# S5 operations merged into wider ones, softmax normalisation on another engine, and six projection rows spread over eight attention heads

## The chip, the cores and the metric

The kernel runs on one NeuronCore of a Trainium2 chip. The metric is the device time of one execution in microseconds; the time of the kernel before is the median of three runs. A NeuronCore has five engines that work side by side: TensorE (PE, matrix products from SBUF into PSUM; PEld is its weight load), VectorE (DVE), ScalarE (ACT), GpSimd (POOL) and SyncE (SP, which issues the weight transfers). Each engine executes its own instructions in order and waits for others through semaphores.

## The reference, cut to what matters

Two layers of a streaming encoder on 272 tokens (16 meta tokens and 256 frames) of width 2048. The change touches only the mixer of the first layer. It projects the tokens once, gives 1024 columns to a diagonal state-space model (S5) and the rest to eight heads of latent attention, and projects both results back:

```python
proj = h @ w_in
a_out = s5_mixer(proj[..., :o1], ...)
b_out = mla_mixer(proj[..., o1:o2], proj[..., o2:o3], proj[..., o3:], ...)
return jnp.concatenate([a_out, b_out], axis=-1) @ w_out
```

S5, per group of 16 channels with 64 complex states, is a linear recurrence over the tokens; `f` is a complex factor of each state that scales `b`:

```python
bb_re = f_re[..., None] * b_re - f_im[..., None] * b_im
bb_im = f_re[..., None] * b_im + f_im[..., None] * b_re
...
_, _, s_re, s_im = lax.associative_scan(_complex_affine_combine, (a_seq_re, a_seq_im, bu_re, bu_im), axis=0)
y = einsum(s_re, c_re) - einsum(s_im, c_im)
y = y.reshape(bsz, n, S5_WIDTH) + d * u
g = jax.nn.gelu(y)
return g * jax.nn.sigmoid(g @ w_glu)
```

Each attention head is a softmax over the visible keys, times the values. Feed-forward networks and a second layer (Mamba-2) follow; nothing in them changes.

## The kernel before, in words

**Matrix products.** Every projection is computed by `linear` (L138). Weights are streamed through `weights` (L112) in chunks of 128 x 1024 (eight tiles of 128 x 128): a DMA into a staging tile `st` (four buffers), a cast by ACT into the high part `hi` (L129), the remainder `lo` by DVE (L130); `hi` and `lo` have three buffers each. Each tile then takes three matmuls of 272 columns (L176, L177, L178). The order of instructions on each engine is set by a scheduler that simulates a timeline over the whole program, so the code order is only its input.

**The stage around the change** is `layer0_mixer` (L591). It computes part of the input projection (`in0b`), the S5 constants (`S5.setup`), the rest of the latents (`in0a`), the q up-projection `uq`, S5 run 0, the k up-projection, the values, S5 run 1, and then a loop over eight heads. For each head h, `scores` (L783) of head h+1 is written first: six matmuls into two banks (`sc_a`, `sc_b`), masks, row maxima (L805, DVE), scaling of the maxima (L806), the exponential (L807, ACT), the reciprocal of the sum (L808) and the normalisation (L809, DVE). `values` (L813) then transposes the probabilities of head h (`pt_a`, L824), copies them (L829) and multiplies by the values (`att_o`, L832). The scores, `pt_a` and the rope share three PSUM banks. After the heads 0 to 5, one row of the input projection (`in0_2` to `in0_7`, 16 tiles, 48 matmuls each) is computed; its result is copied to u by ACT (L669) and starts an S5 run. Heads 6 and 7 have no row.

**One S5 run** (`S5.run`, L1302; q is its number) sends the row of u to memory and back in shifted form (`u2`), multiplies it by `gt` into two PSUM tiles (`w_p`, L1320), turns them by the tables `ec` and `es` (L1326 to L1331, DVE), scans over time (L1337, L1338), turns them back (L1339 to L1345), and computes the output `s5y_p` from u with `kb` (L1350, the local part) and from the states with `ca` (L1354); u is then overwritten (L1357). `w_p`, `s5y_p`, `gt_p` and `kb_p` share two PSUM banks. After that, `prep_pe` (L1267) of run q+1 makes `gt` (transposes L1277, copies L1279), `kb` (L1284, L1289) and the tables, and `prep` (L1234) of run q+2 makes on POOL the constants `gb` and `ca` (products L1256 to L1261, copied by ACT at L1264 and L1265). `cmul` (L1067) is a complex product of six operations; POOL uses it in `prep` and DVE in `prep_pe`, with the same three scratch buffers, of which one is also used by `zsqr` (L1103) in the setup.

**After the heads**, `split` (L209) casts the eight head outputs into `mix`, the second half of the output projection (`out0b`) runs with its evacuation on DVE, ACT applies the GELU to the eight rows of u (after the last head's output), and `glu` and `out0a` follow.

## Time and profile before

| | before |
|---|---|
| median of 3 runs | 2657.0 us (2655.68 to 2657.4) |
| profiled execution | 2660.51 us |
| its span, from first to last instruction | 2658.5 us |
| mean granted TensorE clock | 0.995 |
| instructions | 48273 |

In a row of the profile, a name such as `w_p L1320` is the tile that an instruction writes and its line in the kernel; `x8` is a count. "A <- B" in a list of waits says that instruction A stood still until B was done. A window row gives the busy time of each engine in a stretch of the span, with the granted TensorE clock (1.00 is full speed) and the transfer rate. The stage of the change lies between about 64 and 255 us of the span.

### The profile page before, as it was taken

Reading aid. Unit: us, or ns where it says so; the run is one execution under the profiler, and the core shown is the slowest. Engines: PE = TensorE matmul, PEld = TensorE weight load, DVE = VectorE, ACT = ScalarE, POOL = GpSimd, SP = SyncE. Lnnn points to the kernel's source line nnn. Section 1 sums busy time; section 2 is a strip of 40 time slices with the busy share of each in tenths; the row PEclk is TensorE's granted clock in tenths of the full one; section 3 lists DMA queues with packets and bytes.
Section 4 is the critical chain, followed back from the end, with each engine's and each line's share of the span. In section 5 each row is a group of like instructions: output and inputs, shape, how many; then the busy total and the mean of one; then the engine's idle time right before and its main releaser. Section 6 shows DMA issues by size and latency. Waiting matters only on the chain.

```text
span 2658.5 us, 48273 instructions
## 1 busy us (share of the span) xinstructions
PE 2632.5 (99%) x19358; PEld 2464.3 (93%) x19358; DVE 1744.2 (66%) x3035; ACT 1323.7 (50%) x2188; POOL 261.8 (10%) x350
## 2 busy tenths in 40 slices
PE   9999999999999999999999999999999999999999
PEld 9787999999999999999999999999998888888887
DVE  8877597444444445669777875788975555555565
ACT  5555456333333334447655654554664443444453
POOL 2663040000000000210001000001300000000021
PEclk9998999999999999999999999999999999999999
DMA  6333545555555555545655555544565555555553
GB/s 231 123 118 121 168 157 181 177 176 175 175 175 175 175 175 175 175 162 183 208 180 177 180 177 186 179 160 144 182 196 186 188 190 183 189 190 185 188 184 134
DMA packets 140264, 463.97 MB, mean 175 GB/s; under 512 B 14908, under 2 KB 30844, under 8 KB 139912
## 3 DMA queue, kind: packets, MB, share of 16 engines
q1 hardware_dynamic: 139608, 460.40, 52.5%
q8 instruction: 151, 2.47, 0.4%
q14 instruction: 73, 0.60, 0.1%
q10 hardware_dynamic: 432, 0.49, 0.1%
HBM read 457.56 MB, written 3.28 MB: 173 GB/s over the span
## 4 chain that ended last, share of the span: by engine, by line
PE 88%; DVE 7%; POOL 2%; issue 2%; ACT 1%; DMA 0%; SPq 0%; DVEq 0%; ACTq 0%; POOLq 0%
PE mm_gu_b L173 6%; PE mm_gu_a L173 5%; PE mm_in L173 4%; PE mm_gu_a L178 4%; PE mm_gu_a L177 4%; PE mm_gu_a L176 4%; PE mm_gu_b L178 3%; PE mm_gu_b L176 3%; PE mm_gu_b L177 3%; PE mm_gu_b L174 3%; PE mm_dn_b L173 3%; PE mm_dn_a L173 3%; PE mm_in L177 3%; PE mm_in L178 3%; PE mm_in L176 3%; PE mm_gu_a L174 2%
## 5 line engine op out<-in xcount | busy, mean ns | idle before, releaser
L130 DVE TENSOR_TENSOR lo_gu_b<-st_gu_b,hi_gu_b 128x1024 fp32r<-128x1024 f32 x176 | 215.6, 1225 | 228.8 <-ACT hi_gu_b L129 228.7
L130 DVE TENSOR_TENSOR lo_gu_a<-st_gu_a,hi_gu_a 128x1024 fp32r<-128x1024 f32 x176 | 215.2, 1223 | 178.2 <-ACT hi_gu_a L129 177.9
L129 ACT CAST hi_gu_b<-st_gu_b 128x1024 fp32r<-128x1024 f32 x176 | 184.8, 1050 | 290.4 <-issue 155.7
L129 ACT CAST hi_gu_a<-st_gu_a 128x1024 fp32r<-128x1024 f32 x176 | 184.5, 1049 | 234.3 <-issue 116.4
L173 PE MATMUL mm_gu_b<-m,hi_gu_b 128*128 128x512 f32 x704 | 246.8, 395 | 0.0
L130 DVE TENSOR_TENSOR lo_in<-st_in,hi_in 128x512 fp32r<-128x512 f32 (+1 forms) x268 | 182.1, 708 | 77.1 <-ACT hi_in L129 76.2
L129 ACT CAST hi_in<-st_in 128x512 fp32r<-128x512 f32 (+1 forms) x268 | 158.5, 637 | 128.2 <-PE mm_in L177 42.2
L352 POOL TENSOR_TENSOR ln_s<-ln_s,ln_q 128x272 f32<-128x272 f32 (+1 forms) x58 | 71.4, 1231 | 1442.5 <-ACT ln_q L347 1442.0
L178 PE MATMUL mm_gu_a<-mix,lo_gu_a 128*128 128x272 f32 (+1 forms) x704 | 204.3, 291 | 0.3 <-DVE lo_gu_a L130 0.3
L177 PE MATMUL mm_gu_a<-mix,hi_gu_a 128*128 128x272 f32 (+1 forms) x704 | 203.8, 290 | 0.0
L176 PE MATMUL mm_gu_a<-mix,hi_gu_a 128*128 128x272 f32 (+1 forms) x704 | 203.2, 289 | 0.0
L178 PE MATMUL mm_gu_b<-mix,lo_gu_b 128*128 128x272 f32 x704 | 203.2, 289 | 0.0
L177 PE MATMUL mm_gu_b<-mix,hi_gu_b 128*128 128x272 f32 x704 | 202.7, 288 | 0.0
L176 PE MATMUL mm_gu_b<-mix,hi_gu_b 128*128 128x272 f32 x704 | 202.5, 288 | 0.0
L174 PE MATMUL mm_gu_b<-m,lo_gu_b 128*128 128x256 f32 x704 | 197.2, 280 | 0.0
L173 PE MATMUL mm_gu_a<-m,hi_gu_a 128*128 128x512 f32 x544 | 190.7, 395 | 0.0
L173 PE MATMUL mm_in<-f,hi_in 128*128 128x512 f32 x512 | 181.7, 396 | 0.0
L130 DVE TENSOR_TENSOR lo_dn_a<-st_dn_a,hi_dn_a 128x1024 fp32r<-128x1024 f32 x88 | 107.8, 1225 | 110.4 <-ACT hi_dn_a L129 110.0
L129 ACT CAST hi_dn_a<-st_dn_a 128x1024 fp32r<-128x1024 f32 x88 | 92.3, 1049 | 162.1 <-PE mm_dn_a L177 78.5
L173 PEld LDWEIGHTS mm_gu_b<-m,hi_gu_b 128*128 128x128 f32 x704 | 132.5, 188 | 31.2
L130 DVE TENSOR_TENSOR lo_dn_b<-st_dn_b,hi_dn_b 128x1024 fp32r<-128x1024 f32 x88 | 108.6, 1234 | 74.4 <-ACT hi_dn_b L129 74.0
L129 ACT CAST hi_dn_b<-st_dn_b 128x1024 fp32r<-128x1024 f32 x88 | 92.4, 1050 | 130.4 <-PE mm_dn_b L177 48.6
(555 smaller groups left out, 8586.9 us busy)
## 6 DMA issues: line engine op xcount, KB each, us to landing
st_gu_a<-in_w_gu_a SPq DMA_DIRECT2D x176, 512.0 KB, 3.7
st_gu_b<-in_w_gu_b SPq DMA_DIRECT2D x176, 512.0 KB, 4.0
st_in<-in_w_in SPq DMA_DIRECT2D x140, 512.0 KB, 3.3
st_dn_a<-in_w_dn_a SPq DMA_DIRECT2D x88, 512.0 KB, 3.3
st_dn_b<-in_w_dn_b SPq DMA_DIRECT2D x88, 512.0 KB, 3.3
st_in1h<-in_w_in1h SPq DMA_DIRECT2D x34, 512.0 KB, 3.3
st_out1a<-in_w_out1a SPq DMA_DIRECT2D x32, 512.0 KB, 3.3
st_out0b<-in_w_out0b SPq DMA_DIRECT2D x16, 512.0 KB, 3.8
```

Of the source, the lines that this page charges most:

```text
L129: nc.scalar.copy(hi[:, j:j + w], st[:, j:j + w])
L130: nc.vector.tensor_tensor(lo[:, j:j + w], st[:, j:j + w], hi[:, j:j + w], op=ALU.subtract)
L173: nc.tensor.matmul(ps[m].rearrange("p (a b) -> p a b", a=2), lhsT=wh, rhs=x2, start=st, stop=False)
L174: nc.tensor.matmul(o, lhsT=wl, rhs=xh, start=False, stop=left[m] == 0)
L176: nc.tensor.matmul(o, lhsT=wh, rhs=xh, start=st, stop=False)
L177: nc.tensor.matmul(o, lhsT=wh, rhs=xl, start=False, stop=False)
L178: nc.tensor.matmul(o, lhsT=wl, rhs=xh, start=False, stop=left[m] == 0)
L352: nc.gpsimd.tensor_tensor(st["s2"], st["s2"], q, op=ALU.add)
```

## The change

There are four parts.

- **The loop over the heads.** Rows still follow heads, but the two heads without a row are now 1 and 4 instead of 6 and 7: head 0 has row 2, head 1 none, head 2 row 3, head 3 row 4, head 4 none, and heads 5, 6 and 7 have rows 5, 6 and 7.
- **The normalisation** of the probabilities moves from DVE (`tensor_scalar`) to ACT (`mul`), 24 operations.
- **S5 preparation.** The factor `f` is multiplied into the powers once, in the setup (`fw`, for all 32 states at once), and no longer into `c` in each `prep`. With it go `cmul` and the negated copy `nci`; ACT negates when it copies instead. The fourth power of `gb` (which is one) is copied from `bc` and not multiplied. `zs` gets a buffer of its own, `m4x` becomes one tile for all runs.
- **S5 run.** The two tables become one tile `tab` with three planes (cos, sin, minus cos). A turn is then two products of 544 columns and a sum of 544 (`turned`) instead of four products of 272 and two sums; a run has two turns. The table itself is four products and two sums into `tab`, and a negation by ACT.

The core of the diff:

```diff
@@ layer0_mixer
-                if h < 6:
-                    self.linear(f"in0_{h + 2}", rhs, evac_u, N)
+                if h not in (1, 4):
+                    self.linear(f"in0_{2 + h - (h > 1) - (h > 4)}", rhs, evac_u, N)
@@ scores
-            nc.vector.tensor_scalar(p, p, z, None, op0=ALU.mult)
+            nc.scalar.mul(p, p, z)
@@ S5.zsqr
-        t = self.t("zs", [64], tag="cm2", bufs=1).rearrange("p (r a) -> p r a", r=2)
+        t = self.t("zs", [64], bufs=1).rearrange("p (r a) -> p r a", r=2)
@@ S5.setup
+        fw = self.t("fw", [2, 5, 32])
+        t1, t2 = (self.t(f"fw{c}", [2, 5, 32], tag=f"cm{c}") for c in range(2))
+        for t, c in ((t1, fr), (t2, fi)):
+            v.tensor_tensor(t, pw, c.unsqueeze(1).unsqueeze(1).to_broadcast([P, 2, 5, 32]), op=ALU.mult)
+        v.tensor_tensor(fw[:, 0], t1[:, 0], t2[:, 1], op=ALU.subtract)
+        v.tensor_tensor(fw[:, 1], t1[:, 1], t2[:, 0], op=ALU.add)
@@ S5.prep
-        self.cmul(g, cr, ci, bc[:, :, 2, :], bc[:, :, 3, :], fr, fi, [4, 16])
-        nc.scalar.mul(nci, ci, -1.0)
-        for (o, n, k0, xr, xi, sign) in ((gb, 4, 1, ...), (ca, 5, 0, cr, ci, -1)):
+        for (o, z, k0, n, c) in ((gb, self.pw, 1, 3, 0), (ca, self.fw, 0, 5, 2)):
...
+                if c:
+                    nc.scalar.mul(o[hs, 1, :, 0:n, h, :], t3[hs], -1.0)
+                else:
+                    nc.scalar.copy(o[hs, 1, :, 0:n, h, :], t3[hs])
+                    nc.scalar.copy(o[hs, :, :, 3, h, :], bc[hs, :, 0:2, :].rearrange("p s r j -> p r s j"))
@@ S5.prep_pe
-        self.cmul(g, ec..., es..., gr, gi, er, ei, [4, 9, 8])
+        for r, t in ((0, t1), (1, t2)):
+            e = self.ez[:, r, s].unsqueeze(2).to_broadcast([P, 4, 9, 8])
+            for c in range(2):
+                g.tensor_tensor(t[:, c], gz[:, c].unsqueeze(3).to_broadcast([P, 4, 9, 8]), e, op=ALU.mult)
...
+        nc.scalar.mul(tab[:, 2], tab[:, 0], -1.0)
@@ S5.run
-        v.tensor_tensor(a1, w[0], c, op=ALU.mult)
-        v.tensor_tensor(a2, w[1], s, op=ALU.mult)
-        v.tensor_tensor(b1, w[1], c, op=ALU.mult)
-        v.tensor_tensor(b2, w[0], s, op=ALU.mult)
-        v.tensor_tensor(a1, a1, a2, op=ALU.add)
-        v.tensor_tensor(b1, b1, b2, op=ALU.subtract)
...
+        def turned(o, re, im):
+            v.tensor_tensor(a1, re.unsqueeze(1).to_broadcast(sh), tab[:, 0:2, :, 0:68], op=ALU.mult)
+            v.tensor_tensor(a2, im.unsqueeze(1).to_broadcast(sh), tab[:, 1:3, :, 0:68], op=ALU.mult)
+            v.tensor_tensor(o, a1, a2, op=ALU.add)
+        turned(a1, w[0], w[1])
+        for r in range(2):
+            v.tensor_tensor_scan(z[:, r]..., m4..., a1[:, r]..., 0.0, ALU.mult, ALU.add)
+        turned(z, z[:, 0], z[:, 1])
```

What the scheduler makes of it shows at three places. Before, on PE, behind row 4 (the first line is its last matmul) came the end of the values of head 2 and, between pieces of the next S5 run (`kb_p` and the first half of `w_p`), the scores of head 4 (all but the last scores line is shown); row 5 began eight lines further on:

```order
L178 MATMUL mm_in_4_4_2422<-h_82,lo_in_4_1_2450 128x272
L832 MATMUL att_o<-pt,v 128x272
L832 MATMUL att_o<-pt,v 128x192
L832 MATMUL att_o<-pt,v 128x64
L793 MATMUL sc_a<-qk 80x80
L1284 MATMUL kb_p<-ca_548,gb 32x128 x8
L1320 MATMUL w_p<-u_2210,gt 128x68 x4
L794 MATMUL sc_a<-kr,qrope 80x80
L793 MATMUL sc_a<-qk 128x208
L794 MATMUL sc_a<-kr,qrope 128x208
L793 MATMUL sc_b<-qk 64x272
```

Now, on PE, a piece between row 4 and row 5, where head 4 has no row (`sc_a` are now the scores of head 6, `s5y_p<-ro,ca` are the state products of run 3, `u_2429` is row 4 and belongs to run 4):

```order
L1265 MATMUL gt_p<-ident,gb 128x128 x4
L1339 MATMUL s5y_p<-ro_2197,ca_554 32x67 x32
L1272 MATMUL kb_p<-ca_550,gb 32x128 x8
L1313 MATMUL w_p<-u_2429,gt 128x68 x8
L794 MATMUL sc_a<-qk 80x80
L795 MATMUL sc_a<-kr,qrope 80x80
L794 MATMUL sc_a<-qk 128x208
L795 MATMUL sc_a<-kr,qrope 128x208
L1335 MATMUL s5y_p<-u,kb_551 128x272
L1335 MATMUL s5y_p<-u,kb_551 128x68x3
L1335 MATMUL s5y_p<-u,kb_551 128x68x2
L1335 MATMUL s5y_p<-u,kb_551 128x68
```

Two S5 runs and the scores and values of two heads now stand between these rows; row 5 begins 13 lines after the last one shown.

On DVE, before, run 3 (the tiles `ro`, `vr`, `vi`) with the softmax of a head beside it:

```order
L1327 TENSOR_TENSOR ro_2226<-w_p,es 128x272
L1328 TENSOR_TENSOR ro_2227<-w_p,ec 128x272
L1330 TENSOR_TENSOR ro_2225<-ro_2225,ro_2226 128x272
L808 RECIPROCAL sm<-sm 128x1
L1331 TENSOR_TENSOR ro_2227<-ro_2227,ro_2228 128x272
L808 RECIPROCAL sm<-sm 64x1
L1337 SCALAR_TENSOR_TENSOR vr<-m4x_550,ro_2225 128x272
L809 TENSOR_SCALAR prob<-prob,sm 128x208
L1338 SCALAR_TENSOR_TENSOR vi<-m4x_550,ro_2227 128x272
L809 TENSOR_SCALAR prob<-prob,sm 64x272
L1339 TENSOR_TENSOR ro_2225<-vr,ec 128x272
L1340 TENSOR_TENSOR ro_2226<-vi,es 128x272
```

The same run on DVE now, in the stretch without a row (`lo_in_6_0` is the remainder of the first chunk for row 6, `L1327` are the two scans):

```order
L1321 TENSOR_TENSOR ro_2195<-w_p,tab 128x544
L1322 TENSOR_TENSOR ro_2196<-w_p,tab 128x544
L130 TENSOR_TENSOR lo_in_6_0_2918<-st_in_6_0_2915,hi_in_6_0_2917 128x1024
L1323 TENSOR_TENSOR ro_2195<-ro_2195,ro_2196 128x544
L800 MEMSET sc_a 16x64
L1327 SCALAR_TENSOR_TENSOR ro_2197<-m4x,ro_2195 128x272 x2
L806 TENSOR_REDUCE mx<-sc_a 80x1
L806 TENSOR_REDUCE mx<-sc_b 64x1
L1321 TENSOR_TENSOR ro_2195<-ro_2197,tab 128x544
L1322 TENSOR_TENSOR ro_2196<-ro_2197,tab 128x544
L1292 COPY m4x<-m_437 128x4x67
```

The normalisations (L809 before) are gone from DVE there; the wider products L1321 and L1322 each stand for two.

At the end of the heads, on ACT, before: the last output of a head (`qk`), the table load and the GELU, and the casts of the first chunks of `out0b`:

```order
L1289 COPY kb_549<-kb_p 32x4x32 x4
L834 COPY qk<-att_o 128x272
L754 ACT_TABLE_LOAD
L754 ACTIVATE u<-u 128x272 x7
L210 CAST mix<-qk 128x272
L210 CAST gh<-u 128x272 x4
L210 CAST gl<-u 128x272 x3
L129 CAST hi_out0b_3511<-st_out0b_3509 128x1024
L129 CAST hi_out0b_3543<-st_out0b_3541 128x1024
L129 CAST hi_out0b_3575<-st_out0b_3573 128x1024
```

And now, where row 7 is still to be evacuated (L669) and runs 6 and 7 to be fed (`tab`, `ca`, `gt`, `gb`) when the GELU of the first rows begins:

```order
L755 ACT_TABLE_LOAD
L755 ACTIVATE u<-u 128x272 x5
L129 CAST hi_out0b_3283<-st_out0b_3281 128x1024
L210 CAST gh<-u 128x272 x4
L210 CAST gl<-u 128x272
L1291 ACTIVATE tab<-tab 128x288
L1248 COPY ca_554<-pp_2849 64x20x16 x2
L1267 COPY gt<-gt_p 128x512
L1252 COPY gb<-pp_2835 64x4x3x16 x2
L755 ACTIVATE u<-u 128x272
L129 CAST hi_out0b_3315<-st_out0b_3313 128x1024
L669 COPY u<-mm_in_7_7_3104 128x272
```

The casts of the head outputs (`mix<-qk`, L210) were spread before and now follow as a group of eight right behind the last line shown.

## The prediction

> **What bounds the kernel now.** First the page's busy times and the throttle row of its 40 slices.

> ```profile
> PE 2632.5 (99%) x19358; PEld 2464.3 (93%) x19358; DVE 1744.2 (66%) x3035; ACT 1323.7 (50%) x2188; POOL 261.8 (10%) x350
> PEclk9998999999999999999999999999999999999999
> ```

> TensorE (PE) is busy 99% of the span. Neither kernel changes its matmuls, only their order, so the change can win or lose only PE's idle time and PE time at a reduced clock. One slice shows a reduced clock, the fourth (199 to 266 us): the end of the stage that the diff touches. So next come PE's waits from 60 to 340 us, which spans S5, attention and the start of the output projection (waited-for instruction, us in total, times, longest):

> ```profile
> PE mm_uq L176 <- ACT qk L690: 2.4, 1, 2.4
> PE w_p L1320 <- ACT kb L1289: 2.0, 2, 1.6
> PE w_p L1320 <- DVE mx L806: 2.0, 1, 2.0
> PE rope_sw L632 <- ACT rope_x L630: 1.5, 1, 1.5
> PE s5y_p L1354 <- DVE vr L1344: 0.9, 1, 0.9
> PE s5y_p L1350 <- DVE sm L808: 0.9, 1, 0.9
> PE mm_out0b L178 <- DVE lo_out0b L130: 0.2, 1, 0.2
> ```

> These are all of them: 9.9 us. 3.9 us are early (q up-projection and rope); 5.8 us lie at the bare heads 6 and 7. Then the clock, by windows of 10 us and one of 1 us (window, its length, busy us of PE, PEld, DVE, ACT and POOL, granted clock, DMA share, GB/s):

> ```profile
> 75.00:85.00 10.00, 7.60 (x66) 6.82 (x65) 9.75 (x14) 5.90 (x12) 10.00 (x13) 1.00 0.21 62
> 215.00:225.00 10.00, 5.53 (x103) 3.98 (x102) 9.20 (x26) 3.03 (x11) 5.93 (x8) 0.91 0.20 62
> 225.00:235.00 10.00, 9.02 (x33) 7.09 (x33) 9.78 (x28) 5.95 (x19) 4.40 (x6) 0.50 0.23 58
> 235.00:245.00 10.00, 10.00 (x124) 8.82 (x125) 1.83 (x5) 5.86 (x16) 0.00 (x0) 0.74 0.01 2
> ...
> 223.00:224.00 1.00, 0.00 (x0) 0.00 (x0) 0.78 (x5) 0.00 (x0) 0.92 (x3) 0.59 0.00 0
> ```

> The clock falls to half at about 223.2 us (0.59 is a fifth of the window at 1.00, the rest at 0.50) and stays there through 225 to 235 us, where DVE, busy 9.78 of 10, feeds PE too slowly; half of the next window is still at half clock, though PE has no gap there. Work at half clock takes twice as long: 9.02 / 2 = 4.5 us lost there, 10 x (1 - 0.74) = 2.6 behind it, 0.3 before 225, together 7.4. With the waits that makes **17.3 us of loss** in this stage. It is the most that the change can win; everything after 254 us is gapless PE.

> **The change part by part.** *Spreading the heads.* The bare tail (heads 6 and 7 with S5 runs 5 and 6 and no matmuls to fill) loses 5.8 + 7.4 = 13.2 us. One row is 48 matmuls. Two inner pairs now lose theirs: (1,2) and (4,5), the latter holding S5 runs 3 and 4. What bounds a pair is the chain on DVE and ACT per head against PE's work. The rows:

> ```profile
> L130 DVE TENSOR_TENSOR lo_in<-st_in,hi_in 128x1024 fp32r<-128x1024 f32 x12 | 15.0, 1248 | 8.4 <-ACT hi_in L129 8.3
> L129 ACT CAST hi_in<-st_in 128x1024 fp32r<-128x1024 f32 x12 | 12.6, 1047 | 4.7 <-PE mm_in L177 3.1 <-ACT hi_in L129 0.8 <-DMA st_in<-in_w_in 0.6
> L805 DVE TENSOR_REDUCE mx<-sc_a 128x1 f32<-128x208 f32 x8 | 2.9, 360 | 0.0
> L807 ACT ACTIVATE prob<-sc_a,mx 128x208 f32<-128x208 f32 x8 | 3.5, 433 | 3.7 <-DVE mx L806 3.6
> L1337 DVE TENSOR_TENSOR_SCAN vr<-m4x,ro 128x272 f32<-128x272 f32 x8 | 7.0, 880 | 0.0
> L1082 DVE TENSOR_TENSOR cm<-gz,ez 128x288 f32<-128x288 f32 x8 | 7.6, 945 | 0.0
> ```

> Pair (1,2), counted from the end of row 2's matmuls: the two casts of the next weight chunk come first, because a slot of three is freed there (1.05 ACT, then 1.22 DVE), then reductions and exponentials of head 2 (0.4 + 0.4, three times, in part side by side). The scores of head 3 need the bank that head 2's 128x208 exponential reads; it comes free at about 5.2 us, and PE, with head 2's transposes and the S5 work at hand, gets there at 3.55: **1.7 us idle** (0.5 if the casts hide, 4 if both score banks are late).

> Pair (4,5): the S5 chain is rebuilt from 272-wide into 544-wide operations. No row has that width. Two consecutive quiet 272-wide products start 0.36 us apart:

> ```profile
> 216.08 0.43 DVE L1341 TENSOR_TENSOR ro<-vr,es 128x272 f32<-128x272 f32 x1
> 216.44 0.43 DVE L1342 TENSOR_TENSOR ro<-vi,ec 128x272 f32<-128x272 f32 x1
> ...
> L1330 DVE TENSOR_TENSOR ro<-ro,ro 128x272 f32<-128x272 f32 x8 | 5.1, 636 | 0.0
> L1326 DVE TENSOR_TENSOR ro<-w_p,ec 128x272 f32<-128x272 f32 x8 | 3.5, 432 | 5.8 <-PE w_p L1320 5.8
> ```

> So 544 costs between 0.36 (nothing for the width) and 2 x 0.64 = 1.27 (the slower row twice); I take 0.63, 0.36 and three quarters of it again, near the quiet rows. Both sides of run 3, counted from the end of row 4's matmuls, need PE's own stretches (windows cut at the timeline's starts: the scores of a head, the local S5 product s5y_p, a head's first five transposes; then the gt transposes):

> ```profile
> 212.59:215.41 2.82, 2.82 (x14) 1.00 0.47 176
> 206.59:207.80 1.21, 1.21 (x10) 1.00 0.03 5
> 199.17:199.89 0.72, 0.72 (x8) 1.00 0.00 0
> ...
> 215.41 0.66 PE L1277 MATMUL gt_p<-ident,gb 128*128 128x128 f32 x4
> 217.48 0.33 PE L1354 MATMUL s5y_p<-vr,ca 128*32 128x67 f32 x8 [0.93 <-DVE vr L1344]
> 221.26 1.24 PE L1320 MATMUL w_p<-u,gt 128*128 128x68 f32 x8 [1.55 <-ACT kb L1289]
> 224.45 1.98 PE L1320 MATMUL w_p<-u,gt 128*128 128x68 f32 x8 [1.96 <-DVE mx L806]
> ```

> DVE, in the order of the new program: casts 1.05 + 1.22 + 0.13 between, sum 0.63, two scans of 0.71 (0.36 twice; the group's 0.88 holds stretched ones), two reductions 0.67, two products 1.26, table copy and small operations 0.48, sum 0.63 = 7.5 us. PE has 2.82 + 0.72 + 1.21 and two gt groups of 0.5 (0.66 less its overlapped end) = 5.75 until the state products (the 217.48 row's kind): **1.75 idle**. Then DVE does a reciprocal, four table products and two sums at about 0.46, a reduction and the u update, 3.6 us, until 11.1; only that frees the PSUM bank for the next w_p. PE's state products and kb_p, 1.85 (from 217.48 to 221.26 less the wait of 1.55 and the transposes between, 0.38), end at 9.35: **1.75 idle**. Together 3.5, from 1 (544 at its low end) to 6.4 (the six table operations at 945 instead of 460 ns, 2.9 more). In both waits PE stands in order: behind them are kb_p, w_p(4), head 6's scores and row 5, and behind w_p(4) run 4's whole DVE chain.

> *Normalisations and shared buffers.* The rows of what goes (first three the normalisations, then waits for scratch that DVE and POOL share):

> ```profile
> L809 DVE TENSOR_SCALAR prob<-prob,sm 128x208 f32<-128x208 f32 x8 | 4.5, 557 | 0.1
> L809 DVE TENSOR_SCALAR prob<-prob,sm 64x272 f32<-64x272 f32 x8 | 3.7, 460 | 0.1
> L809 DVE TENSOR_SCALAR prob<-prob,sm 80x80 f32<-80x80 f32 x8 | 2.9, 367 | 0.0
> DVE cm L1081 <- POOL cr L1083: 6.1, 6, 3.5
> POOL cm L1082 <- DVE wz L1108: 16.0, 1, 16.0
> ```

> 24 normalisations, 4.5 + 3.7 + 2.9 = 11.1 us, go from DVE to ACT: per head 1.4 off the one and on the other. ACT, busy 5.95 of 10 us in the window where DVE is 9.78, has the room; if ACT is what PE waits for, it costs up to 1.4 per pair, within the bounds above. DVE's 6.1 us and POOL's 16.0 us of waits end, as do POOL's six 64-wide operations per prep; its gb products shrink from 256 to 192 elements, and ACT gets four small copies or negations instead of one, off PE's path like the rest of a prep that has a whole head to finish. One m4x and one set of tables instead of two or more cost nothing: DVE, which writes them, is also the one that reads them, in order. The weight loads and the u transfers move with their rows, onto queues that are used 0.20 to 0.23 in these windows. The setup gains two DVE products of 320 and two sums of 160 elements, by the rows above 0.25 to 0.45 each, 1.4 us together, hidden by the matmuls of in0a (no wait of PE names its weights); uncovered it would cost its 1.4. Of the early 3.9 us, where ACT's copies were late in a window with DVE and POOL full (9.75 and 10.00), I leave **1.5** (0, if the shorter queues remove it, to 6, if the products add to it).

> *The tail.* Row 7 now stands behind head 7, so run 6's update of u, the GELU and the mix casts of the eight heads come while row 7's and out0b's matmuls run.

> ```profile
> L754 ACT ACT_TABLE_LOAD x1 | 1.3, 1283 | 0.0
> ```

> ACT's queue after the last head is: table load 1.3, five GELUs, a weight cast 1.05, five casts, tables, gt copies, then the eight mix casts that out0b's first matmul needs. kb_p(6) waits 1.0 for u (like the 0.93 of the 217.48 row), w_p(6) 0.9 for the gt copy (between 0.4 and 1.6, the two waits for ACT's kb copies in the list), out0b 1.1 for the casts, the state products of run 6, now among out0b's matmuls, 1.0 to 1.3: **4.0**, from 1 to 6. Run 7 and the gated unit behind it have the last 217 matmuls of out0b as cover, 17 us at the rate of the 235 to 245 window; without it the 5 to 6 us of a run would show.

> *Sum.* 1.5 + 1.7 + 3.5 + 4.0 + 0.5 (small gaps of the kind of the 0.2 row) = 11.2 us, against 17.3: **-6.1 us**. The profiled execution took 2660.51 us (2.0 around its span of 2658.5) and would take 2654.4; it lies 3.5 above the median of the runs, 2657.0, which goes to **2650.9**.

> **Rivals.** *R1, the clock falls in the pair (4,5).* At 223.2 it fell after 3.5 us of idle within 4.75 us (the last two w_p rows: 1.55 and 1.96 with one w_p half between); in the window 75 to 85 PE stood 2.4 us in one piece and kept 1.00. My pair loses 3.5 us within 5.35, 1.85 us of work between: near the edge, on the safe side. If it falls, what follows w_p(4) runs at half: the same operations as from 224.45 to 235 before (0.55 and 9.02 us at half, 4.8 at full clock) and a head's scores, 2.8: +7.6; and the way back costs 2.6 as in the 235 to 245 window: +10.2, 2661.1, and with the table operations slow (2.9) 2664.0. This is the slower side; it decides when the two waits of the pair, with little between, sum to more than 3.5 us within 4.75. [...] Chance of R1 0.30, half of it within 0.2%, half slower.

> *R2, more is gained.* 544-wide near 0.4 and ACT never late: pair and tail halve, 1.5 + 0.8 + 1.8 + 2.0 = 6.1: -11.2, about 2645.8. For it: DVE loses 11.1 us of normalisations and 6.1 of waits. Against: the chain is serial. 0.14.

> *R3, the change does not do what it says.* The stalls only move into the pairs; DVE stays the bound at 9 of 10 us, and the sum stays near 17: 2657 +- 3. 0.14. [...]

> **How the numbers follow.** Forecast 0.42 (its own range 2646 to 2655), R1 0.30, R2 0.14, R3 0.14. 0.2% is 5.3 us, about what a measurement of this kernel tells from no change: below 2651.7 is faster. Of the forecast 0.27 is faster, 0.15 same; R2 is faster; R3 same; R1 0.15 same and 0.15 slower: 0.41, 0.44, 0.15. The range goes from R2's far half (2643) to R1's upper end (2664).

> **What would show it.** Right: no window below clock 1.00 between 60 and 350 us; PE waits of 1 to 2 us at s5y_p(3) and w_p(4); out0b starting 6 us earlier. Wrong: a 0.50 window in the pair (4,5) (R1); the L1321 products above 0.9 us, or the table products still at 0.9 (R3); PE waits beyond 15 us in total. A wait of PE for ACT's prob, a kind that the list does not have, would say that ACT took over from DVE as the bound.

## The result, and the profile after

The changed kernel took 2676.4 us (median of 4 runs, 2675.93 to 2678.67) against 2657.0 before: 19.4 us slower, ratio 1.0076 (95% interval 1.006 to 1.0092). The forecast was 2650.9. The profiled execution has a span of 2674.7 us, 16.2 more than before.

First, from the page of the changed kernel, busy times and the throttle row:

```profile
PE 2641.6 (99%) x19358; PEld 2472.5 (92%) x19358; DVE 1733.8 (65%) x2967; ACT 1339.1 (50%) x2228; POOL 224.0 (8%) x301
PEclk9989999999999999999999999999999999999999
```

The matmuls are as many as before, but PE is busy 9.1 us longer: work at a lower clock (mean granted 0.990 against 0.995). DVE has 10.4 us less to do and POOL 37.8, as the change says; neither made TensorE faster. Next, TensorE's waits from 60 to 340 us (us in total, times, longest):

```profile
PE mm_in0a L178 <- DVE lo_in0a L130: 4.7, 1, 4.7
PE w_p L1313 <- DVE mx L807: 3.8, 1, 3.8
PE sc_a L794 <- ACT prob L808: 2.2, 1, 2.2
PE w_p L1313 <- DVE ro L1321: 0.8, 1, 0.8
PE kb_p L1272 <- DVE u L1342: 0.7, 1, 0.7
PE s5y_p L1339 <- DVE ro L1323: 0.7, 1, 0.7
PE w_p L1313 <- ACT gt L1267: 0.7, 1, 0.7
PE mm_uq L176 <- ACT qk L690: 0.6, 1, 0.6
PE gt_p L1265 <- DVE ro L1322: 0.6, 1, 0.6
PE vp L713 <- ACT qk L697: 0.5, 1, 0.5
PE gt_p L1265 <- ACT gt L1267: 0.3, 1, 0.3
```

They come to 15.6 us, against 9.9 before, and the first is new: the last weights of in0a. The clock, by windows (length, busy us of PE, PEld, DVE, ACT, POOL, granted clock, DMA share, GB/s): the setup, pair (1,2), pair (4,5) and the tail:

```profile
55.00:65.00 10.00, 6.29 (x49) 6.03 (x48) 8.63 (x17) 5.95 (x13) 8.86 (x12) 1.00 0.23 68
65.00:75.00 10.00, 9.05 (x60) 9.05 (x61) 10.00 (x27) 5.23 (x10) 2.89 (x3) 0.83 0.50 144
135.00:145.00 10.00, 8.15 (x64) 5.99 (x58) 4.16 (x11) 6.33 (x16) 4.85 (x8) 0.99 0.36 98
145.00:155.00 10.00, 9.65 (x29) 5.98 (x30) 2.39 (x13) 5.05 (x19) 1.17 (x2) 0.50 0.34 89
155.00:165.00 10.00, 10.00 (x51) 9.21 (x51) 8.01 (x15) 2.15 (x7) 0.22 (x1) 0.66 0.01 2
185.00:195.00 10.00, 6.42 (x108) 4.43 (x108) 9.98 (x21) 5.50 (x17) 5.21 (x5) 1.00 0.43 124
195.00:205.00 10.00, 8.85 (x32) 7.34 (x32) 6.32 (x15) 3.90 (x13) 5.01 (x8) 0.55 0.05 14
245.00:255.00 10.00, 8.50 (x58) 8.02 (x49) 8.30 (x19) 9.03 (x26) 1.63 (x2) 0.66 0.53 161
```

In these two profiles the clock falls four times instead of once between 12 and 330 us. From such windows, 1 us wide, a "clock loss" can be summed: PE's busy time times one minus the granted clock.

| stretch of the changed kernel | PE idle, us | clock loss, us |
|---|---|---|
| setup, 60 to 75 us | 4.7 | 1.7 |
| pair (1,2), 140 to 163 | 2.2 | 8.2 |
| pair (4,5), 184 to 208 | 4.7 | 5.0 |
| tail, 240 to 256 | 2.2 | 3.1 |
| all, 12 to 330 | 15.8 | 18.0 |
| the kernel before, 12 to 330 | 10.0 | 7.4 |

Idle time grew by 5.8 us and clock loss by 10.6, together 16.4: nearly the difference of the two spans, 16.2. **Two thirds of the loss is half clock.** In pair (1,2), 2.2 us of waiting cost another 8.2 us of slow work. The clock loss is an estimate: it takes work at half clock to last twice as long, as the forecast did, and the matmuls of a row, which start 0.13 us apart at full clock and 0.23 us apart behind pair (1,2), last 1.8 times as long.

### The profile page after: what moved, and what is told of

The parts are those of the page before. It is cut to its first block, busy times and chain, and to the rows that moved or that the text cites. A ratio compares the mean times of both kernels' runs of the same rounds, so it can differ in the third digit from the quotient of the medians.

```text
span 2674.7 us, 48162 instructions
## 1 busy us (share of the span) xinstructions
PE 2641.6 (99%) x19358; PEld 2472.5 (92%) x19358; DVE 1733.8 (65%) x2967; ACT 1339.1 (50%) x2228; POOL 224.0 (8%) x301
## 4 chain that ended last, share of the span: by engine, by line
PE 89%; DVE 6%; ACT 1%; issue 1%; DMA 0%; POOL 0%; DVEq 0%; ACTq 0%; POOLq 0%
PE mm_gu_b L173 6%; PE mm_gu_a L173 5%; PE mm_in L173 4%; PE mm_gu_a L178 4%; PE mm_gu_a L177 4%; PE mm_gu_a L176 4%; PE mm_gu_b L178 3%; PE mm_gu_b L176 3%; PE mm_gu_b L177 3%; PE mm_gu_b L174 3%; PE mm_dn_b L173 3%; PE mm_dn_a L173 3%; PE mm_in L177 3%; PE mm_in L178 3%; PE mm_in L176 3%; PE mm_gu_a L174 2%
## 5 line engine op out<-in xcount | busy, mean ns | idle before, releaser
L130 DVE TENSOR_TENSOR lo_gu_b<-st_gu_b,hi_gu_b 128x1024 fp32r<-128x1024 f32 x176 | 215.7, 1225 | 228.7 <-ACT hi_gu_b L129 228.6
L130 DVE TENSOR_TENSOR lo_gu_a<-st_gu_a,hi_gu_a 128x1024 fp32r<-128x1024 f32 x176 | 216.4, 1230 | 178.3 <-ACT hi_gu_a L129 177.8
L129 ACT CAST hi_gu_b<-st_gu_b 128x1024 fp32r<-128x1024 f32 x176 | 184.8, 1050 | 290.4 <-issue 155.6
L129 ACT CAST hi_gu_a<-st_gu_a 128x1024 fp32r<-128x1024 f32 x176 | 184.4, 1049 | 234.8 <-issue 116.4
L130 DVE TENSOR_TENSOR lo_in<-st_in,hi_in 128x512 fp32r<-128x512 f32 (+1 forms) x268 | 184.3, 716 | 95.1 <-ACT hi_in L129 93.8
L129 ACT CAST hi_in<-st_in 128x512 fp32r<-128x512 f32 (+1 forms) x268 | 158.5, 637 | 129.5 <-PE mm_in L177 39.8
L178 PE MATMUL mm_gu_a<-mix,lo_gu_a 128*128 128x272 f32 (+1 forms) x704 | 204.6, 291 | 0.3 <-DVE lo_gu_a L130 0.3
L177 PE MATMUL mm_gu_a<-mix,hi_gu_a 128*128 128x272 f32 (+1 forms) x704 | 203.6, 289 | 0.0
L178 PE MATMUL mm_gu_b<-mix,lo_gu_b 128*128 128x272 f32 x704 | 203.2, 289 | 0.0
L176 PE MATMUL mm_gu_a<-mix,hi_gu_a 128*128 128x272 f32 (+1 forms) x704 | 202.9, 289 | 0.0
L177 PE MATMUL mm_gu_b<-mix,hi_gu_b 128*128 128x272 f32 x704 | 202.7, 288 | 0.0
L176 PE MATMUL mm_gu_b<-mix,hi_gu_b 128*128 128x272 f32 x704 | 202.4, 288 | 0.0
L130 DVE TENSOR_TENSOR lo_dn_a<-st_dn_a,hi_dn_a 128x1024 fp32r<-128x1024 f32 x88 | 107.8, 1225 | 110.4 <-ACT hi_dn_a L129 110.0
L129 ACT CAST hi_dn_a<-st_dn_a 128x1024 fp32r<-128x1024 f32 x88 | 92.3, 1049 | 162.1 <-PE mm_dn_a L177 78.5
L129 ACT CAST hi_dn_b<-st_dn_b 128x1024 fp32r<-128x1024 f32 x88 | 92.4, 1050 | 130.0 <-PE mm_dn_b L177 48.6
L130 DVE TENSOR_TENSOR lo_dn_b<-st_dn_b,hi_dn_b 128x1024 fp32r<-128x1024 f32 x88 | 108.6, 1234 | 74.0 <-ACT hi_dn_b L129 73.6
```

The costliest lines, as they stand in the source:

```text
L129: nc.scalar.copy(hi[:, j:j + w], st[:, j:j + w])
L130: nc.vector.tensor_tensor(lo[:, j:j + w], st[:, j:j + w], hi[:, j:j + w], op=ALU.subtract)
L176: nc.tensor.matmul(o, lhsT=wh, rhs=xh, start=st, stop=False)
L177: nc.tensor.matmul(o, lhsT=wh, rhs=xl, start=False, stop=False)
L178: nc.tensor.matmul(o, lhsT=wl, rhs=xh, start=False, stop=left[m] == 0)
```

## The experiments

Theory A: TensorE's clock halves after stalls far shorter than the prediction allowed (2.2 us in pair (1,2), against its 3.5 us within 4.75), and the spread of the heads made two more such stalls. Theory B took the other side in each run. Clock losses and idle times below are sums like those of the table, from 12 to 330 us of each profile.

**One part at a time.** First the loop over the heads alone; then everything but that loop; then each of the rest's two parts alone: the normalisation on ACT, and the S5 rework.

```diff
# heads alone: the kernel before, with the new loop
-                if h < 6:
+                if h not in (1, 4):
# rework: the changed kernel, with the old loop
# normalisation alone: the kernel before, with
+            nc.scalar.mul(p, p, z)
# S5 alone: the rework, with
+            nc.vector.tensor_scalar(p, p, z, None, op0=ALU.mult)
```

> The kernel before with the new loop over the heads alone. Theory A (the clock: the new pairs (1,2) and (4,5) stall TensorE long enough to halve its clock, whatever S5 looks like): both pairs show a 0.50 stretch, together 12 us or more of clock loss, the bare tail's 13 us are gone but for 2 to 5; no stall in the setup: 2662 to 2672. Theory B (the S5 rework does the harm, the spread of the heads is a gain as forecast): no 0.50 stretch in the pairs, 2646 to 2653.

> All of the change but the loop over the heads, which is as before (heads 6 and 7 bare). Theory A: the stall of the setup stays (4.7 us of wait for lo_in0a and 1.7 at half clock, against 3.9 of early waits before), the bare tail falls to half clock as before: 2655 to 2663. Theory B (the rework slows DVE and POOL everywhere): 2668 or more.

> The kernel before, with nothing changed but the 24 normalisations on ACT. Theory A (the rework's 10 us come from the setup and S5): DVE has 11.1 us less, the bare tail's chain is a little shorter: 2652 to 2657. Theory B (ACT, which now waits for the reciprocal of DVE 24 times in its order, holds up casts and copies): 2662 or more.

> The kernel before with the S5 rework alone: normalisations on DVE, heads 6 and 7 bare. Theory A: it holds most of the 10 us of the rework run: wait for lo_in0a of 4 to 5 us, half clock behind it, and the bare tail: 2663 to 2669. Theory B: 2655 to 2659.

| run | median, us | ratio to before, 95% interval | idle | clock loss |
|---|---|---|---|---|
| heads alone | 2665.7 | 1.0031 (1.002 to 1.0042) | 9.3 | 16.9 |
| rework | 2667.0 | 1.0035 (1.002 to 1.0049) | 12.7 | 17.7 |
| normalisation alone | 2663.1 | 1.003 (1.0019 to 1.0042) | 13.5 | 4.3 |
| S5 alone | 2673.8 | 1.0066 (1.0051 to 1.0081) | 17.0 | 14.1 |

Idle time and clock loss are those of one profiled execution each. Those of heads alone and of the rework took 3.0 and 6.6 us more than the medians beside them.

Every part alone is slower. The spread of the heads is the cleanest: it waits no longer than the kernel before (9.3 against 10.0), and what its profile loses more, 9.5 us, is all clock loss. Its windows show the fall in the pair (1,2):

```profile
135.00:145.00 10.00, 6.62 (x33) 3.91 (x32) 5.50 (x16) 6.05 (x16) 8.35 (x10) 0.91 0.62 172
145.00:155.00 10.00, 10.00 (x36) 7.00 (x36) 3.56 (x16) 2.38 (x10) 0.00 (x0) 0.50 0.01 2
155.00:165.00 10.00, 10.00 (x43) 8.97 (x43) 6.33 (x16) 1.14 (x3) 3.44 (x8) 0.57 0.06 15
```

TensorE is busy without a gap from 145 to 165 us, and at half clock until 163.7. Theory B fell here. The rework came out 4 us above the expected range of A and 1 us below that of B: it has the setup's stall (4.6 us), and its bare tail is no better than before. S5 alone is 5 us above the expected range of A, so more than the setup and the old tail is slow in it. The normalisation alone was expected to be harmless and is 7 us slower: TensorE now waits for ACT's copies and for out0b's evacuation, as these lines of its list of waits show, which the kernel before does not have:

```profile
PE mm_out0b L176 <- DVE x L745: 1.7, 1, 1.7
...
PE att_o L832 <- ACT pt L829: 1.3, 1, 1.3
```

The parts do not add up (9 + 10 gives 19.4, but 7 + 18 is not 10). Each also gives the scheduler another order, which may be why; that was not tried.

**Filling the stalls.** If it is the clock, then work added in the stall must make the kernel faster. Dense matmuls whose product is read by nobody were put into the pairs, each behind the transposes of the bare head:

```diff
+                if h in (1, 4):
...
+                    with tc.issue_after(self.tp.ins):
+                        for _ in range({1: 17, 4: 30}[h]):
+                            nc.tensor.matmul(fl[:, :N], lhsT=hx[:, 0, 0, :P], rhs=hx[:, 1, 0, :N], start=True, stop=True)
```

> The changed kernel with 17 more matmuls of a row's kind (2.15 us) put on TensorE exactly where it stalls 2.2 us in pair (1,2), ahead of the scores of head 3; their product is read by nobody. The order on TensorE is otherwise the same up to the output projection. Theory A (two thirds of the loss is half clock after a stall): the stretch of 17 us at 0.50 behind that stall goes, and with it 8.2 us: about 2668, although work was added. Theory B (the time goes with the waits themselves): the wait is replaced by as much work and the time stays at 2676.

> As the run with 17 filling matmuls, and 30 more (3.8 us, 23 and 6 and 1 around the second group of gt transposes) in the pair (4,5), ahead of the state products of run 3, where TensorE has 0.97 us of small stalls and then 3.76 us behind kb_p. What DVE does until w_p(4) may start does not hang on TensorE there. Theory A: no stretch at 0.50 in either pair; against the run with one fill 3 to 7 us less, against the changed kernel 8 to 14 less: 2662 to 2669. Theory B (waits, not the clock): as slow as the changed kernel or slower by the part of the 3.8 us that does not fall into a stall: 2676 to 2680.

With 17 matmuls in pair (1,2): 2672.0 us (ratio to before 1.0055, 1.004 to 1.007), 4.4 less than the changed kernel. With 47: **2661.4 us** (1.0021, 1.0012 to 1.003), 15 less, with 5.9 us of work more. The windows of the run with 47 over both pairs:

```profile
135.00:145.00 10.00, 10.00 (x64) 7.43 (x63) 4.46 (x13) 6.80 (x20) 5.67 (x8) 1.00 0.52 148
145.00:155.00 10.00, 10.00 (x65) 8.16 (x65) 7.49 (x20) 4.13 (x15) 0.00 (x0) 1.00 0.15 41
185.00:195.00 10.00, 9.92 (x96) 7.35 (x85) 5.25 (x19) 9.21 (x33) 3.74 (x6) 1.00 0.06 16
195.00:205.00 10.00, 9.67 (x129) 8.80 (x127) 9.89 (x14) 3.60 (x9) 6.88 (x7) 1.00 0.01 2
```

No window is below 1.00, and the clock loss is 1.7 us in all, that of the setup. TensorE's idle time fell by 6.9 us, about what the filling matmuls take (5.9), and the clock loss by 16.3, so the gain is the clock. This profile is of the fastest of ten executions (2658.9, the slowest took 2665.3); the median gained less. In the run with 17 the stretch at half clock behind pair (1,2) is gone as well:

```profile
140.00:150.00 10.00, 9.98 (x55) 6.25 (x54) 5.34 (x22) 5.26 (x20) 5.69 (x8) 1.00 0.61 174
150.00:160.00 10.00, 10.00 (x83) 9.14 (x84) 8.92 (x16) 4.70 (x14) 1.94 (x2) 1.00 0.01 2
190.00:200.00 10.00, 10.00 (x32) 6.74 (x32) 5.93 (x14) 2.19 (x9) 5.01 (x8) 0.50 0.01 2
```

It gained 4.4 instead of 8 because the pair (4,5), still unfilled, had a clock loss of 8.5 us there instead of 5.0 (14.1 in all, against 18.0). The same filling with the old S5 asks what the spread is worth without the clock:

> The kernel before with the new loop over the heads alone (2665.7), and filling matmuls in both pairs: 26 (3.3 us) in the 3.4 us stall ahead of the scores of head 3, 12 (1.5 us) behind the transposes of head 4, where 1.2 us are idle. Theory A: both 0.50 stretches (10.2 and 3.4 us in that profile) go: 2652 to 2655, below both kernels. Theory B: 2664 to 2667.

> The same with the 26 matmuls in the pair (1,2) alone. Theory A: 10 us less than the spread heads alone, the pair (4,5) falls to half clock or not by the phase of the grid (1.2 us idle): 2653 to 2659. Theory B: 2664 to 2667.

26 matmuls in pair (1,2): 2656.2 us, 9.5 below the heads alone and the same as before (1.0001, 0.9992 to 1.001). 12 more in (4,5): 2658.7 (1.0009, 1.0 to 1.0017); its profile has another fall, at 215 us, in a stretch without a filler. The first lies inside theory A's range for it, the second 4 us above; both are far below that of B. So with its stalls filled the spread of the heads is as fast as the kernel before and no faster; the whole change was forecast to win 6 us.

```diff
+                if h == 0:
...
+                    for _ in range(4):
+                        nc.tensor.matmul(fl[:, :N], lhsT=hx[:, 0, 0, :P], rhs=hx[:, 1, 0, :N], start=True, stop=True)
```

> The changed kernel with four more matmuls of a row's kind (0.5 us) ahead of row 2, whose product nobody reads. In the changed kernel the clock changes only at 66.2, 69.6, 144.7, 161.8, 195.9, 206.1, 247.1 and 253.9 us, all on one grid of 3.413 us, and the 2.2 us stall of pair (1,2) lies 1.55 to 0.65 over a grid point. Theory A (a grid stretch with more than about 1.4 us idle halves the clock): moved by 0.5 us the stall splits 1.05 to 1.15 and the clock stays at 1.00 in pair (1,2): that stage loses 8.2 us less although work was added; the pair (4,5) idles longer than two such shares and still falls. Theory B (it falls after any stall of 2 us or more): a 0.50 stretch of 10 us or more in pair (1,2) as without the addition, and 0.5 us more in all.

2676.5 us, with a fall in pair (1,2) as without the four matmuls. It tells the theories apart less than was meant, since the grid had moved: its changes lie at a remainder of 0.42 us from multiples of 3.413, not 1.35, and of the 2.2 us stall 1.6 lay in one stretch. Behind that pair its order had changed too (21.0 us idle and 13.5 of clock loss, against 15.8 and 18.0), so the equal time says little. Therefore each kernel was profiled once more:

> The changed kernel once more, for a second profile. Theory A with a free grid: the clock's changes lie again on one grid of 3.413 us, but at another remainder than 1.34 us, and the idle times are the same as in the first profile within 1 us in sum while the half-clock loss differs by up to one grid stretch per stall. If the grid is fixed to the program's start, the remainder is 1.34 again.

> The kernel before once more, for a second profile: as above; with a free grid the half-clock loss of the bare tail is 4 to 9 us, and the early stall of 2.4 us may halve the clock, which it did not in the first profile.

The remainders are 1.90 us, against 1.35 in the first profile of the changed kernel, and 0.17, against 1.32 in that of the kernel before: the grid is free, it lay elsewhere in the second execution of either kernel. The changed kernel's idle time is the same (15.9 and 15.8 us), its clock loss 20.5 instead of 18.0. The kernel before, second profile, and then stretches between grid points, two of its first profile (76.41 to 83.24) and two of its second:

```profile
75.00:85.00 10.00, 7.60 (x58) 7.18 (x57) 9.10 (x13) 5.90 (x12) 10.00 (x13) 0.85 0.26 82
...
225.00:235.00 10.00, 9.02 (x43) 7.50 (x43) 9.72 (x27) 7.04 (x22) 4.50 (x6) 0.64 0.22 58
235.00:245.00 10.00, 10.00 (x141) 9.21 (x141) 4.49 (x13) 8.12 (x24) 0.00 (x0) 1.00 0.10 15
...
76.41:79.83 3.41, 2.13 (x25) 1.70 (x23) 3.41 (x6) 2.25 (x6) 3.41 (x5) 1.00 0.27 60
79.83:83.24 3.41, 2.30 (x18) 2.30 (x19) 3.41 (x5) 3.07 (x6) 3.41 (x6) 1.00 0.24 96
...
78.67:82.09 3.41, 1.26 (x10) 1.26 (x11) 3.41 (x8) 3.37 (x7) 3.41 (x7) 1.00 0.47 156
82.09:85.50 3.41, 3.41 (x17) 3.22 (x15) 2.51 (x3) 0.70 (x2) 3.41 (x5) 0.50 0.40 131
```

The early stall of 2.4 us, which kept 1.00 in the first profile, now halves the clock: in the first a grid point split it into 1.3 and 1.1 us, in the second 2.2 us of it lie in one stretch. The tail is back at full speed at 232 us instead of 240: 8.5 us idle and 5.5 clock loss, 3.4 us less than in the first profile (10.0 and 7.4), as its span is (2655.1 against 2658.5). Between the two second profiles idle time grows by 7.4 us and clock loss by 15.0, so two thirds is half clock here too; together that is more than the spans differ (19.8), as the clock loss is somewhat overstated.

Over the 19 profiles (two of each of these kernels and one of every other run), the falls and rises of the clock between 55 and 300 us lie on such a grid, each profile with a remainder of its own (0.14 to 3.26 us); every stretch between its points reads 1.00 or 0.50. The stretches between grid points that were at full clock, sorted by TensorE's idle time in them:

| idle in one 3.41 us stretch | stretches | clock halved at its end |
|---|---|---|
| under 0.5 us | 1082 | 1 |
| 0.5 to 1.0 | 56 | 10 |
| 1.0 to 1.4 | 26 | 3 |
| 1.4 to 1.8 | 19 | 13 |
| 1.8 to 2.4 | 16 | 14 |
| over 2.4 | 18 | 18 |

From 1.4 us on, 45 of 53 stretches ended in half clock. Idle time doesn't decide alone, as the second and third rows show. There the clock went with what TensorE did otherwise: of the 82 stretches with 0.5 to 1.4 us idle, 44 held 1 us or more of the matmuls of `linear`, and none of them halved the clock; of the other 38, mostly with scores, transposes and S5 products, 13 did.

**No head bare.** The twelve half rows were dealt over eight heads as 2, 1, 2, 1 and so on, with S5 and normalisation of before; with the changed ones; with POOL held as in e3 below; and with the normalisation on ACT alone:

```diff
+                for i in range(3 * h // 2 + h % 2, 3 * (h + 1) // 2 + (h + 1) % 2):
+                    m, c = 2 + i // 2, i % 2
...
+                    for k in range(8 * c, 8 * c + 8):
```

> The kernel before, with S5 and the normalisation as they were, and the twelve half rows dealt over all eight heads (2, 1, 2, 1 ... chunks of eight tiles per head), so that no head is bare. Theory A: no 0.50 stretch between 100 and 235 us, and of the 13.2 us that the bare tail loses 2 to 5 are left: 2646 to 2650. Theory B (the heads' chains on DVE and ACT are late wherever the rows lie): 2655 or more.

> The changed kernel with the half rows dealt in the same way. Theory A: the two pairs' losses (2.2 + 8.2 and 4.7 + 5.0 us) go, the setup's (4.7 + 1.7) and about half of the tail's 5.3 stay: 2655 to 2660. Theory B (the S5 rework is what is slow): 2668 or more.

> As the run before, and POOL's first constants held until the end of the setup by the shared buffer, as in the held run. Theory A: the setup's wait (4.7 us) falls to about 1 and the early waits of 2 to 4 us come back: 2650 to 2658, 1 to 4 us below the run before. If holding POOL only moves the stall it is the same within 2 us.

> The candidate: the kernel before with half rows dealt over all heads and the normalisations on ACT, S5 as it was. Theory A: against the half-row run (2657.5) DVE's 1.4 us per head go, the out0b waits of 3.7 us shrink: 2652 to 2656, below both kernels. Theory B (ACT becomes late, as its casts of mix stand in the same queue): 2657 to 2661.

2657.5 (1.0001, 0.9992 to 1.0011), 2659.4 (1.0009, 1.0 to 1.0019), 2662.0 (1.002, 1.0011 to 1.003) and 2656.9 us (1.0004, 0.9994 to 1.0013). With the changed S5, half rows take back 17 of the 19.4 us. None beats the kernel before. The first was expected at 2646 to 2650: its clock loss fell to 2.8, but TensorE then waited 3.7 us for the mix casts ahead of out0b, a wait that the kernel before does not have. The third was expected no slower than the second and is 2.6 us slower; the fourth was expected at 2652 to 2656. No version of this study is faster than the kernel before.

**The setup.** TensorE waits 4.7 us for lo_in0a. ACT, POOL and DVE there (start, length, operation, in brackets the idle time ahead of it):

```profile
47.78 1.05 ACT L129 CAST hi_in0a<-st_in0a 128x1024 fp32r<-128x1024 f32 x1 [0.75 <-PE mm_in0a L177]
54.55 0.71 ACT L1248 COPY gb<-pp 64x192 f32<-64x192 f32 x2 [5.71 <-POOL pp L1242]
55.28 1.05 ACT L129 CAST hi_in0a<-st_in0a 128x1024 fp32r<-128x1024 f32 x1
...
49.50 4.14 POOL L1241 TENSOR_TENSOR pp<-pw,bc 128x192 f32<-128x192 f32 x1 [1.54 <-DVE rs_t L259]
...
57.88 0.85 DVE L1081 TENSOR_TENSOR zm<-ez,wz 128x128 f32<-128x128 f32 x1
58.66 0.85 DVE L1082 TENSOR_TENSOR zm<-ez,wz 128x128 f32<-128x128 f32 x1
```

The weight cast stands on ACT behind a copy that waits 5.7 us for POOL, one of whose products takes 4.14 us; and DVE's operations beside POOL take 0.85 us (in the kernel before, with POOL standing still, products of this width took 0.28). Two runs each removed one part: e3 shares a buffer again, so that POOL, after its first products, stands still for 8.4 us beside the rest of the setup's chain, while ACT still waits 4.4 us for the first copy; e13 lets POOL do the first copies itself.

```diff
# e3
+        t = self.t("zs", [64], tag="pp3").rearrange("p (r a) -> p r a", r=2)
# e13
+            cp = g.tensor_copy if q == 0 else nc.scalar.copy
```

> The changed kernel, but the setup's scratch zs shares the buffer pp3 with POOL's products, so that POOL's first constants wait for the end of the setup's chain, as they did before. If POOL's early products are what delays the last weights of in0a, the 4.7 us wait and the 1.7 us at half clock behind it go, and some of the early waits of before (up to 3.9) come back: 2671 to 2676, and DVE's small setup operations are back at 0.2 to 0.3 us. If the setup is late for the added fw operations or the normalisations, the wait stays at 4 to 5 us and the time at 2676. The stall positions against the clock's grid move, so the later stages may lose other amounts.

> The changed kernel with the copies of the first constants (run 0's gb and ca, 10 small operations) on POOL instead of ACT; the order on TensorE is unchanged. Theory A (the weight cast of in0a stands on ACT behind the copy that waits 5.7 us for POOL): the casts come on time, lo_in0a's wait falls from 4.7 to 1 us or less, and the half clock behind it goes, 4 to 6 us less: 2670 to 2673; the pairs' stretches stay. Theory B (DVE itself is late, because POOL's products slow its setup operations): the wait stays at 3 us or more and the time at 2674 to 2678.

2679.4 us (1.008, 1.0065 to 1.0095) and 2677.6 (1.0079, 1.0062 to 1.0096). Both removed the wait at in0a (0.8 us are left in e3, nothing in e13), and neither won time. So ACT's wait for POOL and DVE's slow operations beside POOL both had a part in it. In e13's list of TensorE's waits, from 55 to 340 us, the first line is:

```profile
PE mm_uq L176 <- ACT qk L690: 7.5, 2, 6.5
```

The wait moved from in0a to the q up-projection. In e3 the setup did get faster: most of DVE's small operations are back at 0.2 to 0.3 us, as expected, and from 45 to 100 us TensorE is idle for 4.6 us without any clock loss, against 5.9 and 1.7 in the changed kernel. It lost more than that behind: a `w_p` at 117 us now waits 1.9 us for ACT's `kb` and is followed by 6.8 us at half clock, and the stretch at half clock in the pair (4,5) is 13.7 us long instead of 10.2. What sets the end of the setup once in0a no longer waits was not settled.

## Why the prediction was wrong, point by point

**The step that failed** is the sum: it took everything in the pairs, in the setup and in the tail at full clock, and entered 11.2 us against the 17.3 of before. Of before's 17.3 the half clock was 7.4; the forecast entered none of it again. Measured were 15.6 us of waits and 18.0 of clock loss. The reason given was the condition of rival R1: that it takes more than 3.5 us of idle within 4.75 us, because the trace had one stall of 2.4 us that kept 1.00. That was one sample of a free grid; the same stall halved the clock in the second profile. In the 19 profiles 1.4 us of idle in one stretch of 3.41 us were enough in 45 of 53 cases. The pair (4,5) fell by R1's own condition, with 3.8 us of idle in one piece; the pair (1,2), with 2.2, is where that condition fails. R1's mechanism was right, in more places than the one it named. Its price for the pair (4,5), 10.2 us, is twice the 5.0 measured there; 8.2 came at the pair (1,2), where nothing was entered.

**Pair (1,2).** 1.7 us idle were forecast, at the scores of head 3 and for the exponential of head 2: 2.2 measured, at that instruction. Right, but for the 8.2 behind it. The forecast's own sign that ACT had taken over as the bound, a wait for ACT's `prob`, is this very wait, and ACT itself stood 2.3 us there for DVE's row maxima; so the sign does not show what it was meant to.

**Pair (4,5).** 3.5 us forecast (1 to 6.4); 4.7 measured, 0.3 at the gt transposes, 0.7 at the state products and 3.8 at w_p, where 1.75 were forecast. The 544-wide operations, forecast 0.63 us from start to start, are right; these rows have durations of 0.72 with the overlapped end:

```profile
L1321 DVE TENSOR_TENSOR ro<-w_p,tab 128x544 f32<-128x544 f32 x7 | 5.0, 720 | 8.2 <-PE w_p L1313 8.2
190.84 3.83 DVE L1286 TENSOR_TENSOR tb<-gz,ez 128x288 f32<-128x288 f32 x4
194.87 0.44 DVE L1289 TENSOR_TENSOR tab<-tb,tb 128x288 f32<-128x288 f32 x1
190.04 1.30 POOL L1240 TENSOR_TENSOR pp<-fw,bc 128x320 f32<-128x320 f32 x1 [3.98 <-ACT gb L1248]
```

The four table products took 3.83 us there, 0.96 each, the upper bound of the forecast and the sign that it named for R3. POOL's products for a later run went on beside them, from 190.04 to 194.35; the two sums behind them took 0.44 each. Four times 0.96 instead of 0.46 is 2.0 us, which is what w_p waited more than forecast. That POOL was the reason is read from the times and was not tried here.

**Setup.** The end of POOL's 16 us wait for the shared buffer was entered as a gain or nothing, and 1.5 us were left for all early waits. It was the buffer that had kept POOL away from most of the setup: 5.8 us of early waits and 1.7 of clock loss came instead, and e3, which holds POOL again, has 3 us less there. The fw operations (1.6 us), said to be hidden, stand in that chain. How much of it is theirs was not tried.

**Normalisation.** Moving it to ACT was entered as hidden, with up to 1.4 us per pair; alone it costs 7 us.

**Tail.** 4.0 us forecast; 2.2 idle and 3.1 of clock loss, within its bounds of 1 to 6, though not by waits alone. Run 7 and the gated unit are covered, as said: no wait stands behind out0b.

**The median.** The forecast's step from the profiled execution to the median (3.5 us) did not carry over: the changed kernel's profiled execution took 2676.46 us, its median. The 17.3 us of before were those of an execution with an unlucky grid; in the second profile, which took 2657.14, 14.0 were lost. So of the 6.1 us that were taken off the median, some 3.3 were not in it: 11.2 against 14.0 would have given about 2654 by the same sum.

## What to carry to other kernels

Where TensorE is busy 99%, count 1.4 us or more of idle within one such stretch of 3.41 us, behind which the clock halved in 45 of 53 cases here, as its own length plus the slow work behind it, until the clock comes back, which took 3.4 to 20.5 us in these profiles: in pair (1,2) 2.2 us of waiting cost 10.4. Do not take one profile's full clock after a stall as safe, since the grid moves from execution to execution (the early stall of 2.4 us kept 1.00 in one profile of the kernel before and halved the clock in the other); and before spreading bare places over a program, ask how much small work would run at half clock behind each. A buffer that looks like a needless wait may keep two engines apart (in the setup DVE's products of 0.28 us took 0.85 beside POOL); look at what the freed engine will run beside, and at what it is late for when it is held: in e3 holding POOL helped the setup, and the kernel lost more behind it.

## What was not expected of the hardware

A gapless stretch did not suffice to bring the clock back. Behind pair (1,2), TensorE was busy without a gap from 145.35 to 161.8 us; three whole grid stretches of that, with scores, transposes, w_p and the first row matmuls, left it at 0.50, and it came back behind the fourth, which was filled with row matmuls. Of the 129 half-clock stretches in the 19 profiles, it came back behind 59, all with less than 0.5 us idle, but 46 others with as little idle time left it down. All 30 with 3 us or more of the matmuls of `linear` brought it back, and 15 of the 62 with hardly any (under 0.2 us), as in the pair (4,5) at 206.1 us, behind scores and s5y_p. What counts beside idle time is open. And useless work paid: 5.9 us of matmuls that nobody reads made the changed kernel 15 us faster.
